# Two loads ahead of the opening barrier, with new load sizes and shares, in a streaming log-sum-exp

## The chip, the cores and the metric

The kernel runs on 1 core of one Trainium2 chip. The metric is the device time of one execution in microseconds (us). The profile's span, from the first instruction to the last landing, is about 1.8 us shorter than that time. Four comparisons were made, of which the last three ran on three different chips (batches 1 to 3 below). ACT is ScalarE, DVE is VectorE, SP the engine that issues the loads. A load lands when the last of the 16 DMA engines has reported its part; that report is called a completion here.

## The reference, cut to what matters

```python
x = np.random.randn(32, 512, 1024).astype(np.float32)
x_max = np.max(x, axis=-1, keepdims=True)
out = x_max.squeeze(-1) + np.log(np.sum(np.exp(x - x_max), axis=-1))     # (32, 512)
```

There are 16,384 rows of 1,024 floats. Laid over 128 partitions that is 128 rows to a partition. In this text "a row" is one such row on all partitions, 524,288 bytes. The kernel leaves the maximum out, which normally distributed inputs allow.

## The kernel before

Chunks of rows, one load each, are loaded one after the other into a ring of 51 rows. ACT takes the exponential. For the first rows of a chunk it does so in one call, and DVE sums them; for the others it does one call a row in the accumulating form, which sums by itself. A pair `(r, n)` in the list means r rows in the chunk, n of them summed on DVE.

```python
CHUNKS = [
    (4, 1), (15, 11), (16, 10), (16, 15), (16, 0), (14, 0), (12, 9), (9, 5), (7, 5), (5, 4),
    (4, 3), (3, 0), (2, 2), (2, 2), (1, 0), (1, 0), (1, 0),
]
...
    load(0)                                   # moved ahead of the opening barrier below
    n_early = len(body.instructions)
    nc.scalar.preload_act_table_set("natural_log_exp_and_others")
    for i, (r, n_dve) in enumerate(CHUNKS):
        if i:
            load(i)                           # waits until its place in the ring is free
        ...
        nc.scalar.wait_ge(landed[i], 16)
        if n_dve:
            nc.scalar.activation(out=ring[:, s : s + n_dve], in_=ring[:, s : s + n_dve], func=Exp)...
            nc.vector.wait_ge(act_done, acts)
            nc.vector.reduce_sum(out=sums[:, row : row + n_dve], in_=ring[:, s : s + n_dve], axis=AX)...
        for j in range(n_dve, r):
            nc.scalar.activation(out=ring[:, s + j], in_=ring[:, s + j], func=Exp,
                                 accum_out=sums[:, row + j : row + j + 1])...
    ...                                       # Ln of the sums, one store
```

The instructions recorded before `n_early` are put ahead of the barrier that opens the program.

The softmax here doesn't subtract the row's maximum and nothing guards it: scores larger than these inputs give would overflow.

## Time and profile before

| | before |
|---|---|
| time, median of the first 3 runs | 163.2 us (163.04 to 163.21) |
| span of the profiled run | 161.4 us |
| busy: ACT, DVE | 124.1 us, 72.9 us |
| load queue, share of the 16 DMA engines' span | 97.0% |
| last row lands, ACT takes it | 158.21, 158.34 |

The landings to a hundredth are the last of the 16 completions that the trace records for each load. How busy the three parts are, in 40 slices of 4 us, as tenths:

```profile
DVE  0030000029960699000799920000004999799874
ACT  3190006997089980999429999999999999999995
DMA  7999799989989989989989999999899999999990
```

ACT and DVE have holes; the DMA engines have none after the first slice. A digit below 9 in the DMA row comes from packets that lie over the edge of a slice: with each packet's time shared out between the slices that it covers, slices 2 to 39 come to 99% or more. The rest of the reading is in the prediction.

### The profile page before, as it was taken

What the parts mean: (1) busy time and instruction counts of PE and PEld (TensorE: products, weight loads), DVE (VectorE), ACT (ScalarE), POOL (GpSimd) and SP (SyncE); (2) the same over time, 40 slices, a digit from 0 to 9 for tenths busy, and PEclk for the clock granted to TensorE, in tenths of its full rate; (3) what the DMA queues carried; (4) which work ended last, traced back from release to release, by engine and by line L of the source; (5) the groups of instructions that cost most, each with busy time, mean ns of one, the idle gap of its engine ahead of it and who ended that gap; (6) DMA issues with size and microseconds to landing.
All of it is one profiled execution on the core that took longest, in us unless ns stands there. A gap on an engine that the chain in (4) does not pass through costs nothing.

```text
span 161.4 us, 212 instructions
## 1 busy us (share of the span) xinstructions
DVE 72.9 (45%) x11; ACT 124.1 (77%) x136; POOL 0.2 (0%) x4
## 2 busy tenths in 40 slices
DVE  0030000029960699000799920000004999799874
ACT  3190006997089980999429999999999999999995
POOL 0000000000000000000000000000000000000000
DMA  7999799989989989989989999999899999999990
GB/s 264 499 487 442 335 442 520 422 357 520 422 357 520 422 357 520 422 357 520 422 353 426 457 455 422 390 463 475 347 439 434 433 441 402 431 418 416 420 394 24
DMA packets 2593, 67.18 MB, mean 416 GB/s; under 512 B 288, under 2 KB 416, under 8 KB 800
## 3 DMA queue, kind: packets, MB, share of 16 engines
q1 hardware_dynamic: 2448, 67.11, 97.0%
q10 hardware_dynamic: 144, 0.07, 0.1%
q14 instruction: 1, 0.01, 0.0%
HBM read 67.11 MB, written 0.07 MB: 416 GB/s over the span
## 4 chain that ended last, share of the span: by engine, by line
ACT 52%; DMA 38%; DVE 7%; issue 1%
DMA ring<-in_x_dram 38%; ACT ring L127 30%; ACT ring L115 22%; DVE sums L120 7%; ACT res L92 0%
## 5 line engine op out<-in xcount | busy, mean ns | idle before, releaser
L120 DVE TENSOR_REDUCE sums<-ring 128x5 f32<-128x5120 f32 (+8 forms) x11 | 72.9, 6648 | 86.1 <-ACT ring L115 86.0
L115 ACT ACTIVATE ring<-ring 128x5120 f32<-128x5120 f32 (+8 forms) x11 | 59.3, 5395 | 29.6 <-DMA ring<-in_x_dram 29.6
L127 ACT ACTIVATE ring<-ring 128x1024 f32<-128x1024 f32 x61 | 63.4, 1041 | 5.3 <-DMA ring<-in_x_dram 5.3
L127 ACT ACTIVATION_READ_ACCUMULATOR ring<-ring 128x1 f32 x61 | 11.4, 187 | 0.0
L102 ACT ACT_TABLE_LOAD x1 | 1.3, 1283 | 0.8 <-PEq L181 0.8
L92 ACT ACTIVATE res<-sums 128x67 f32<-128x67 f32 (+1 forms) x2 | 0.5, 256 | 0.1
L181 POOL MEMSET const-bfloat16-1.0<- 128x1 bf16 x1 | 0.1, 101 | 0.0
L181 POOL MEMSET const-uint8-127<- 128x1 uint8 x1 | 0.1, 101 | 0.0
L181 POOL MEMSET const-float32-0.0<- 128x1 f32 x1 | 0.1, 98 | 0.2 <-issue 0.2
L181 POOL MEMSET const-float32-1.0<- 128x1 f32 x1 | 0.1, 98 | 0.0
## 6 DMA issues: line engine op xcount, KB each, us to landing
ring<-in_x_dram SPq DMA_DIRECT2D x1, 7680.0 KB, 24.9
ring<-in_x_dram SPq DMA_DIRECT2D x1, 7168.0 KB, 36.0
ring<-in_x_dram SPq DMA_DIRECT2D x1, 6144.0 KB, 21.6
ring<-in_x_dram SPq DMA_DIRECT2D x1, 4608.0 KB, 32.1
ring<-in_x_dram SPq DMA_DIRECT2D x2, 2048.0 KB, 26.3
ring<-in_x_dram SPq DMA_DIRECT2D x1, 3584.0 KB, 40.2
ring<-in_x_dram SPq DMA_DIRECT2D x1, 2560.0 KB, 44.4
ring<-in_x_dram SPq DMA_DIRECT2D x2, 1024.0 KB, 46.0
```

The source lines that it names most:

```text
L92: nc.scalar.activation(out=res[:, lo:hi], in_=sums[:, lo:hi], func=Ln).then_inc(act_done, 1)
L102: nc.scalar.preload_act_table_set("natural_log_exp_and_others")
L115: nc.scalar.activation(out=ring[:, s : s + n_dve], in_=ring[:, s : s + n_dve], func=Exp).then_inc(act_done, 1)
L120: nc.vector.reduce_sum(out=sums[:, row : row + n_dve], in_=ring[:, s : s + n_dve], axis=AX).then_inc(dve_done, 1)
L127: nc.scalar.activation(out=ring[:, s + j], in_=ring[:, s + j], func=Exp, accum_out=sums[:, row + j : row + j + 1],).then_inc(act_done, 1)
L181: nc = _bacc.Bacc("TRN2", target_bir_lowering=False, num_devices=1)
```

## The change

The intent: let the stream of loads open sooner, by a first load of two rows and a second one issued right behind it, and fit the sizes and shares to that.

```diff
 CHUNKS = [
-    (4, 1), (15, 11), (16, 10), (16, 15), (16, 0), (14, 0), (12, 9), (9, 5), (7, 5), (5, 4),
-    (4, 3), (3, 0), (2, 2), (2, 2), (1, 0), (1, 0), (1, 0),
+    (2, 1), (16, 13), (16, 10), (16, 1), (16, 0), (16, 12), (11, 9), (9, 5), (7, 6), (5, 2),
+    (4, 4), (3, 0), (2, 2), (2, 1), (1, 1), (1, 0), (1, 0),
 ]
@@
     load(0)
+    load(1)
     n_early = len(body.instructions)
@@
-        if i:
+        if i > 1:
             load(i)
```

## The prediction

> **What bounds the kernel now.** I read the queue table first, then the chain of work that ended last, the idle time of the engines, the groups kept apart by shape, and last the timeline of the final microseconds and the two loads that open and close the stream.
>
> ```profile
> span 161.4 us, 212 instructions
> DVE 72.9 (45%) x11; ACT 124.1 (77%) x136; POOL 0.2 (0%) x4
> q1 hardware_dynamic: 2448, 67.11, 97.0%
> ```
>
> The load queue holds the 16 DMA engines for 97.0% of 161.4, that is 156.6 us; ACT has 124.1 and DVE 72.9. The input stream is the largest load by far. That alone doesn't say what sets the end, so the chain (start, length, what), cut to the parts up to the point where it turns to ACT for good:
>
> ```profile
> 0.78 24.87 DMA ring<-in_x_dram
> 25.67 9.60 ACT ring L115
> 35.29 11.90 DVE sums L120
> 47.21 36.61 DMA ring<-in_x_dram
> 83.84 10.56 ACT ring L127 x21
> ```
>
> Read plainly, the chain says that the fifth load waited for a DVE reduction (47.21) and that ACT bounds all from 83.84 on. Both readings need a check. The fifth load is issued at 47.21, but the queue then still holds the fourth, which lands only when ACT starts on it at 64.50: that wait is hidden. And ACT's idle time before it, in the groups:
>
> ```profile
> L115 ACT ACTIVATE ring<-ring 128x15360 f32<-128x15360 f32 x1 | 13.0, 13002 | 4.4 <-DMA ring<-in_x_dram 4.4
> L115 ACT ACTIVATE ring<-ring 128x11264 f32<-128x11264 f32 x1 | 9.6, 9589 | 14.0 <-DMA ring<-in_x_dram 14.0
> L115 ACT ACTIVATE ring<-ring 128x10240 f32<-128x10240 f32 x1 | 8.7, 8736 | 5.7 <-DMA ring<-in_x_dram 5.7
> L120 DVE TENSOR_REDUCE sums<-ring 128x15 f32<-128x15360 f32 x1 | 16.2, 16153 | 12.8 <-ACT ring L115 12.8
> L120 DVE TENSOR_REDUCE sums<-ring 128x9 f32<-128x9216 f32 x1 | 9.8, 9753 | 29.6 <-ACT ring L115 29.6
> ```
>
> ACT waits for data before each of the first big chunks, so those starts are landings: 25.67 with 19 rows in, 83.84 (from the chain) with 67 rows in. The slope is 58.17/48 = 1.212 us for a row of 128x1024 floats, 524,288 bytes, or 433 GB/s. Last, the end. The final load's issue, its time to landing, and the timeline there:
>
> ```profile
> 112.46 0.45 SPq L84 DMA_DIRECT2D ring<-in_x_dram  x1
> DMA to landing us min/median/max: 45.8/45.8/45.8
> 158.34 1.04 ACT L127 ACTIVATE ring<-ring 128x1024 f32<-128x1024 f32 x1
> 159.28 0.19 ACT L127 ACTIVATION_READ_ACCUMULATOR ring<-ring 128x1 f32 x1
> 159.50 0.25 ACT L92 ACTIVATE res<-sums 128x61 f32<-128x61 f32 x1
> 159.78 0.37 ACTq L139 DMA_DIRECT2D out_dram<-res  x1
> ```
>
> The last row lands at 112.46 + 45.8 = 158.26 and ACT takes it at 158.34. So ACT arrives within 0.1 us of the data: the stream bounds the kernel, and ACT has been balanced to it. What follows (1.16 us to the logarithm, the logarithm, the store of 1.6 us) is fixed.
>
> **What the Trainium skill says.** "DMA: Bandwidth & Descriptors", section "Where 436 GB/s comes from", puts the ceiling of the 16 ports at 435 GB/s; the 433 above agrees, so no choice of load sizes can gain much. The same page, "Queues, rings and completion order", says each engine consumes its ring in order: a second load issued earlier queues behind the first. The trace agrees, loads land in order of issue. "ScalarE: Activation LUTs", section "What ACT_TABLE_LOAD costs", gives 186 ns + 0.833 ns an element with immediate operands, and an overlap of some 93 ns; for 9216 elements that is 7863, and the trace has 7867. "VectorE: DVE Perf Modes", section "The perf-mode tier table", has the reduction at 1x only; at its 0.96 GHz a row costs 1.067 us, and the trace has (16153 - 9753)/6 = 1067 ns.
>
> **The change, part by part.**
>
> *Both loads ahead of the barrier.* The second load is issued at 0.78 now, with the barrier in front of it. It will be at about 0.4, right after the first one's 0.37 us of issue. The barrier's end, and the table load behind it, come some 0.35 later, which is hidden: ACT then still waits for its first rows. In the windows of the first microseconds (us, the busy shares, then DMA share and GB/s last):
>
> ```profile
> 0.00:1.00 1.00, 0.00 (x0) 0.23 (x1) 0.20 (x4) 1.00 0.00 0
> 1.00:2.00 1.00, 0.00 (x0) 1.00 (x1) 0.00 (x0) 1.00 1.12 262
> 3.00:4.00 1.00, 0.00 (x0) 0.00 (x0) 0.00 (x0) 1.00 1.00 426
> ```
>
> Packets move from about 1 us after the first issue. By the same delay the second load's would be ready from 1.8 to 2.7 with the old issue time, 1.4 to 2.3 with the new. The first load of 4 rows keeps the engines until some 1.3 + 4 x 1.21 = 6.2; of 2 rows, until 3.7. Either way the second is queued in time. The stream's first byte depends on the first load alone, which doesn't move. Gain: 0.
>
> *Load sizes.* The running sum of rows is 2, 18, 34, 50, 66, 82, then 93, 102, 109, 114, 118, 121, 123, 125, 126, 127, 128: from the seventh load on it is the same as before, sizes included. The stream's end stays at 158.26. The new early landings come from the slope: second load at 24.5 (18 rows), third 43.9, fourth 63.3, fifth 82.6, sixth 83.84 + 15 x 1.212 = 102.0.
>
> *Buffers.* A load that waits for a free place costs only if it is issued after the queue has run dry. The tightest are those that need the sixth chunk's place, the first of them being the tenth load (5 rows). The sixth chunk's exponential of 12 rows starts at 102.0 and takes 10.35, the reduction 12 x 1.067 + 0.15 = 13.0, so the place is free at 125.4. By then the queue has work up to 109 rows: 1.3 + 109 x 1.212 = 133.4. Seven to eight us are left, less 1 to 2 for the first packets. The fifth load waits for a reduction of 13 rows to 49.8, against 62 when the queue runs dry. No starvation.
>
> *Shares.* A row by the accumulating form takes 1.04 from start to start; an exponential of n rows takes 0.853 n + 0.115 (start to start: 12.91 for 15 rows, 4.37 for 5). Before: 61 rows at 1.04, 67 rows in 11 calls. After: 62 rows at 1.04, 66 rows in 13 calls. ACT's sum grows by 1.04 - 0.853 + 2 x 0.115 = 0.42 us. Most of it falls where ACT waits. So I follow ACT from the last chunk it waits for. The sixth starts at 102.0 and takes 10.35 + 4 x 1.04, to 116.5; the seventh (9 + 2) takes 7.79 + 2.08, to 126.37; before, ACT came to the eighth at 126.25. Then 5 + 4 rows to 134.91 (134.80 before), 6 + 1 to 141.18 (141.25), 2 + 3 to 146.12 (145.80), 4 + 0 to 149.64 (149.49), 3 single rows to 152.76 (152.60), 2 to 154.58 (154.44), 1 + 1 to 156.59 (156.26), an exponential of 1 to 157.56 (157.30), a single row to 158.60. The last row starts at 158.60, not 158.34: +0.26. The stream is no longer quite last; ACT is 0.3 behind it. DVE's last single-row reduction ends near 159.4 behind the queue of the ones before it, just ahead of the accumulator's 159.7, so it adds nothing.
>
> Sum: 0 (barrier) + 0 (sizes) + 0 (buffers) + 0.26 (ACT's tail) on 163.2 gives 163.46; I say 163.4, as a first load of half the size may open the stream a little sooner.
>
> **The rivals.**
> 1. The early second load does pull the stream forward by the 0.4 us between 0.78 and 0.4, or the smaller first load makes the engines start more evenly, and everything anchored to landings comes forward with it: 163.46 - 0.4, about 163.0. For it: only 262 GB/s moved in the second microsecond, so the start isn't ideal, and somebody chose to do this. Against: full rate by the fourth microsecond with the late issue, and nothing after it for the second load to fill.
> 2. A place comes free too late, at the tenth load: the idle of the queue is then the loss, one for one. It needs DVE 6 us later than worked out, with durations that repeat to 0.1%; if it happened, 164 to 167.
> 3. DVE becomes the tail: its queue of reductions in the last 20 us is dense. It ends 0.3 before ACT by my sum; half a microsecond more on it gives 163.6 to 163.8.
>
> **Range and chances.** The three runs of before spread over 0.17. Rival 1 sets the low end, 162.7 with that spread; rivals 3 and a slip in ACT's tail the high end, 163.9. Two per cent is 3.3 us; faster by that would need the stream to end before 155, at 443 GB/s, above anything the trace shows. Slower by that needs rival 2. Within 2%: 0.98.
>
> **What would show it.** Right: the second issue near 0.4; ACT's start on the second chunk near 24.5 and on the sixth near 102.0; the last load landing within 0.2 of 158.26; ACT's last row starting 0.2 to 0.4 after that landing, with no idle of ACT behind 102. Wrong: an early shift common to all landings (rival 1), a hole in the DMA row of the page after 120 (rival 2), or the final logarithm waiting for DVE (rival 3).

## The result, and the profile after

The changed kernel took 163.51 us, median of 6 runs (163.37 to 163.93), against 163.24 (163.04 to 163.47) for the kernel before beside it. The ratio is 1.0021, 95% interval 1.0006 to 1.0036: the same within 2%. Ratios are the mean time of one kernel's fast runs over that of the other's in the same rounds, so not quite the ratio of the medians. The profiled run, at 163.83, is one of the two slowest of the six; its parts have to be read with that in mind.

The head of its page and its load queue:

```profile
span 162.0 us, 215 instructions
DVE 72.9 (45%) x13; ACT 124.2 (77%) x138; POOL 0.2 (0%) x4
q1 hardware_dynamic: 2448, 67.11, 96.8%
```

Nothing in the totals moved but the span. The start, in windows of one microsecond (DMA share and GB/s are the last two columns), and the second load's issue and landing (the issue line merges the first two):

```profile
1.00:2.00 1.00, 0.00 (x0) 0.75 (x1) 0.00 (x0) 1.00 0.71 205
2.00:3.00 1.00, 0.00 (x0) 0.53 (x1) 0.00 (x0) 1.00 1.02 426
0.00 0.85 SPq L84 DMA_DIRECT2D ring<-in_x_dram  x2
DMA to landing us min/median/max: 23.7/23.7/23.7
```

Both loads are out by 0.85; the second is issued at 0.42 and lands at 24.13. Full rate is there in the third microsecond. ACT's starts on the chunks it waited for are landings, from the timeline:

```profile
24.15 11.30 ACT L116 ACTIVATE ring<-ring 128x13312 f32<-128x13312 f32 x1 [17.21 <-DMA ring<-in_x_dram]
43.53 8.74 ACT L116 ACTIVATE ring<-ring 128x10240 f32<-128x10240 f32 x1 [4.96 <-DMA ring<-in_x_dram]
63.41 1.06 ACT L116 ACTIVATE ring<-ring 128x1024 f32<-128x1024 f32 x1 [4.91 <-DMA ring<-in_x_dram]
83.11 1.06 ACT L128 ACTIVATE ring<-ring 128x1024 f32<-128x1024 f32 x1 [3.07 <-DMA ring<-in_x_dram]
102.46 10.44 ACT L116 ACTIVATE ring<-ring 128x12288 f32<-128x12288 f32 x1 [2.33 <-DMA ring<-in_x_dram]
```

The steps are of 16 rows each: 19.38, 19.88, 19.70, 19.35 us, so 1.211, 1.242, 1.231, 1.209 us a row. The stream opens 0.35 earlier than my 24.5. It then loses 16 x (0.031 + 0.020) = 0.8 us in two loads, which nothing in the prediction foresees. The trace's single packets show how: at about 48, 58 and 68 us 13 of the 16 engines take 2.5 to 2.7 us for a packet of 64 KiB that otherwise takes 2.42. Last, the chain from the sixth chunk on (its first two pieces; all the others up to the final logarithm are ACT's), and the tail:

```profile
63.15 39.29 DMA ring<-in_x_dram
102.46 10.44 ACT ring L116
136.42 0.43 SPq L84 DMA_DIRECT2D ring<-in_x_dram  x1
DMA to landing us min/median/max: 22.2/22.2/22.2
158.89 1.04 ACT L128 ACTIVATE ring<-ring 128x1024 f32<-128x1024 f32 x1
160.06 0.26 ACT L92 ACTIVATE res<-sums 128x62 f32<-128x62 f32 x1
```

From 102.46 ACT has no hole. The last row lands at 158.65 (136.42 + 22.2, to the rounding of that view) and ACT takes it at 158.89, 0.24 later, where the kernel before takes it 0.12 after its landing. The span grew by 0.57; of that, 0.12 is ACT's lateness and 0.44 the later landing.

### The profile page after: what moved, and what is told of

The parts are those of the page before. It is cut to its first block, busy times and chain, and to the rows that moved or that the text cites. A ratio compares the mean times of both kernels' runs of the same rounds, so it can differ in the third digit from the quotient of the medians.

```text
span 162.0 us, 215 instructions
## 1 busy us (share of the span) xinstructions
DVE 72.9 (45%) x13; ACT 124.2 (77%) x138; POOL 0.2 (0%) x4
## 4 chain that ended last, share of the span: by engine, by line
DMA 50%; ACT 41%; DVE 7%; issue 0%
DMA ring<-in_x_dram 50%; ACT ring L116 28%; ACT ring L128 13%; DVE sums L121 7%; ACT res L92 0%
## 5 line engine op out<-in xcount | busy, mean ns | idle before, releaser
L121 DVE TENSOR_REDUCE sums<-ring 128x1 f32<-128x1024 f32 (+8 forms) x13 | 72.9, 5645 | 86.7 <-ACT ring L116 86.7
L116 ACT ACTIVATE ring<-ring 128x1024 f32<-128x1024 f32 (+8 forms) x13 | 59.6, 4591 | 31.7 <-DMA ring<-in_x_dram 31.7
L92 ACT ACTIVATE res<-sums 128x66 f32<-128x66 f32 (+1 forms) x2 | 0.5, 257 | 0.1
```

Source lines behind the costliest of these rows:

```text
L92: nc.scalar.activation(out=res[:, lo:hi], in_=sums[:, lo:hi], func=Ln).then_inc(act_done, 1)
```

## The experiments

Theory: the early issue and the sizes leave the stream as it was, and ACT's tail adds a little. Rivals: the stream opens earlier; the new sizes slow the stream. Because the first profile showed a gain and a loss inside the stream, most runs ask which of the two belongs to the change.

All profiles together. "Second chunk" is ACT's start on it; with 18 rows in, a row (1.21) has to be added to compare it with 19. "Late" is ACT's start on the last row less that row's landing.

| kernel | batch | median us | ratio | second chunk (rows) | last landing | late |
|---|---|---|---|---|---|---|
| before | first | 163.2 | | 25.67 (19) | 158.21 | 0.12 |
| after | first | 163.51 | 1.0021 | 24.15 (18) | 158.65 | 0.24 |
| after_again | 1 | 163.47 | 1.0018 | 24.07 (18) | 158.27 | 0.24 |
| early_only | 1 | 163.18 | 1.0003 | 25.59 (19) | 158.15 | 0.12 |
| sizes_only | 1 | 163.36 | 1.0011 | 24.13 (18) | 158.26 | 0.22 |
| old_tail | 1 | 163.16 | 1.0015 | 24.02 (18) | 157.81 | 0.17 |
| before_again | 2 | 163.58 | 0.9999 | 25.87 (19) | 158.96 | 0.12 |
| small_first | 2 | 163.43 | 0.9992 | 25.56 (19) | 158.49 | 0.13 |
| large_first | 2 | 163.42 | 0.9992 | 24.34 (18) | 158.26 | 0.24 |
| tail_heavy | 2 | 164.29 | 1.0043 | 24.30 (18) | 158.10 | 1.07 |
| before_third | 3 | 163.66 (one run) | | 25.63 (19) | 158.61 | 0.12 |
| after_third | 3 | 163.49 | 1.0012 | 24.17 (18) | 158.63 | 0.25 |
| thin_before | 3 | 162.48 | 0.9951 | 25.68 (19) | 158.06 | 0.02 |
| thin_after | 3 | 162.24 | 0.9940 | 24.16 (18) | 158.50 | 0.02 |

The kernel before had medians of 163.11, 163.59 and 163.28 beside the three batches. So chips alone differ by 0.5 us, more than the effect. In the 12 profiles of kernels that do the whole work, the time of the profiled run is the last landing plus "late" plus 4.93 to 4.96 us. So what is left of a difference in time, once the difference in "late" is taken off, is a difference in the end of the stream.

**after_again.** No edit.

> The changed kernel once more, unedited, to see which features of its one profile come back. In that profile the second load landed 0.3 us nearer the line of 1.21 us a row than before, and between 40 and 75 us the stream then lost 0.7 us that the kernel before does not lose. Theory 1 (the loss is a chance disturbance of the DMA engines): time 163.4 to 163.6, sixth chunk's start on ACT at 101.7 to 102.0 rather than 102.46, and no load slower than 1.22 us a row before the tail. Theory 2 (the loss belongs to the new load sizes): the fourth and fifth loads again take 1.23 to 1.24 us a row and the sixth chunk starts at 102.4 or later.

Measured: 163.47, six runs from 163.01 to 163.87, ratio 1.0018 (1.0004 to 1.0033). The sixth chunk starts at 102.07 and the fifth load takes 1.234 us a row. Both theories missed a part: a slow load came back, but one and not two, in the fifth and not the fourth, and its cost was about half. Neither "never" nor "always" holds.

**early_only.** The kernel before with the second load early:

```diff
     load(0)
+    load(1)
@@
-        if i:
+        if i > 1:
```

> The kernel before with nothing but the second load moved ahead of the barrier. Theory 1 (my prediction: the second load queues behind the first in any case): ratio 1.000 within 0.001, last load lands at 158.1 to 158.3, ACT's start on the second chunk at 25.6 to 25.7. Rival (the early issue is what brought the landings forward by 0.3 us): that start at 25.3 to 25.4, last landing near 157.9, time about 162.9, ratio 0.998.

Measured: ratio 1.0003 (0.9991 to 1.0015), last landing 158.15. The second chunk's start:

```profile
25.59 9.59 ACT L116 ACTIVATE ring<-ring 128x11264 f32<-128x11264 f32 x1 [13.96 <-DMA ring<-in_x_dram]
```

That is 0.08 before the first profile's 25.67, just under my 25.6 to 25.7 and well outside the rival's 25.3 to 25.4. The early issue alone brings at most 0.1 us.

**sizes_only.** The changed kernel with the second load behind the barrier again:

```diff
     load(0)
-    load(1)
@@
-        if i > 1:
+        if i:
```

> The changed kernel with the second load behind the barrier again; sizes and shares stay new. Theory 1 (the early issue is worth nothing): same as the changed kernel, ratio to before 1.001 to 1.003, second chunk's start on ACT near 24.2. Rival (early issue is worth 0.3 us): second chunk's start at 24.45 to 24.55 and the time 0.3 us above the changed kernel, ratio 1.004.

Measured: 163.36, ratio 1.0011 (0.9997 to 1.0025); the second load is issued at 0.77, and yet:

```profile
24.13 11.30 ACT L115 ACTIVATE ring<-ring 128x13312 f32<-128x13312 f32 x1 [17.33 <-DMA ring<-in_x_dram]
```

The start is where the changed kernel has it (24.07 on this chip), so the early issue isn't what brings it. Against early_only, a row added, it is 25.59 - 25.34 = 0.25 earlier: on this chip that belongs to the sizes. This run, too, has a slow load, its seventh, at 1.238 us a row. With that the seventh lands late, and the early start is gone by 115 us.

**old_tail.** The changed kernel with the shares of the last ten chunks of before:

```diff
-(9, 5), (7, 6), (5, 2), (4, 4), (3, 0), (2, 2), (2, 1), (1, 1), (1, 0), (1, 0)
+(9, 5), (7, 5), (5, 4), (4, 3), (3, 0), (2, 2), (2, 2), (1, 0), (1, 0), (1, 0)
```

> The changed kernel with the shares of the last ten chunks put back to those of before (ACT keeps one accumulating row less before the last four single rows). My sum gives ACT's start on the last row at 158.47 if the sixth chunk starts at 102.0, against 158.60 with the new shares and 158.34 before: so about 0.13 us under the changed kernel, ratio to before about 1.001. If ACT's tail is not what ends the kernel, it is equal to the changed kernel within 0.05 us.

Measured: 163.16, but runs from 162.92 to 164.15, ratio 1.0015 (0.9994 to 1.0035). As a time it tells nothing. In the profile ACT is 0.17 late, 0.07 less than with the new shares; my sum had 0.13. In its profile no load of 16 rows takes more than 1.221 us a row, and there the last row lands at 157.81, with a time of 162.92:

```profile
135.60 0.44 SPq L84 DMA_DIRECT2D ring<-in_x_dram  x1
157.98 1.04 ACT L128 ACTIVATE ring<-ring 128x1024 f32<-128x1024 f32 x1
```

So the early start can last to the end, when no slowing takes it back.

**before_again.** No edit.

> The kernel before, unedited, as a control: its second profile shows how far the stream's course differs between executions of one kernel. If the start of the stream is a property of the kernel, the second chunk starts on ACT at 25.6 to 25.7 as in the first profile and the engines' first and last completion of a load lie 0.75 to 0.85 us apart; if it is chance, 25.2 to 25.7 is possible. Time 163.0 to 163.3, ratio 1.000.

Measured: 163.58, ratio 0.9999. The time is above my 163.0 to 163.3, as that of the kernel before beside it is (163.59). The stream of its profile, the slowest of its five runs, is the worst of all: slowings of 6 to 11 engines at 6, 30 and 39 us, the second and third loads at 1.240 and 1.237 us a row, the last landing at 158.96. The second chunk starts at 25.87, outside what I had allowed, and from the third load on the engines' completions of one load lie 1.1 to 1.3 us apart instead of 0.8. The slowings aren't a mark of the new sizes.

**small_first.** The kernel before with another cut of the first two loads:

```diff
-    (4, 1), (15, 11),
+    (2, 1), (17, 11),
```

> The kernel before with the first two loads cut at 2 and 17 rows instead of 4 and 15; all sums from the second load on, all shares but one accumulating row, and the late second issue are those of before. Theory (the smaller first load alone brings all landings forward by 0.3 us): second chunk's start on ACT at 25.2 to 25.35, and if nothing is lost later, the last landing at 157.9 and the time 162.8 to 162.9, ratio 0.998. Rival (the gain is taken back by a common slowing of the DMA engines between 40 and 110 us, as in three of four profiles with the new sizes): same start, but the last landing at 158.1 to 158.6 and the time 163.0 to 163.5, with runs spread over more than 0.5 us.

Measured: 163.43 (163.27 to 163.58), ratio 0.9992 (0.9980 to 1.0005). The second chunk starts at 25.56, so neither expectation of the start was met, and the fourth load is slow (1.245 us a row), so the last landing is the rival's 158.49. The spread of its runs, 0.31, is under the rival's 0.5. One thing besides the cut differs: the load of 17 rows goes in 256 packets of 34,816 bytes, where the other large loads go in 128.

**large_first.** The changed kernel with another cut of the first two loads:

```diff
-    (2, 1), (16, 13),
+    (4, 1), (14, 13),
```

> The changed kernel with the first two loads cut at 4 and 14 rows instead of 2 and 16; the sums are those of the changed kernel from the second load on. Theory (first load's size sets the start): the second chunk starts on ACT at 24.45 to 24.55, not 24.1. If the even start of the small first load is also what makes the engines slow each other down later, this kernel shows no load over 1.22 us a row before the last ten, runs within 0.3 us, last landing 158.2 and the time 163.3 to 163.4 by ACT's tail alone. If the later slowing is independent of it, its runs spread like the changed kernel's, up to 163.9.

Measured: 163.42 (163.33 to 163.51), ratio 0.9992. The second chunk starts at 24.34, earlier than expected, and only 0.04 later than that of tail_heavy, which opens with two rows on the same chip. The fifth load took 1.228 us a row, but that is no common slowing: the packets show one engine alone held up at 72 us, by a fetch of instructions, and the completions of that load lie 0.95 us apart where those of the load before lie 0.65 apart. Apart from that the stream is even, as expected of the first case, and the last landing and lateness are as it said. One even execution doesn't show that the larger first load is the reason, since the kernel before, which also opens with four rows, had slowings in before_again. On this chip the gain of 0.25 us from the smaller first load is not seen; whether it is a matter of the chip or of the execution stays open.

**tail_heavy.** The changed kernel with five rows of the eighth chunk in the other form:

```diff
-(9, 5), (7, 6), (5, 2),
+(9, 0), (7, 6), (5, 2),
```

> The changed kernel with five rows of the eighth chunk moved from exponential plus reduction to the accumulating form. ACT's work in the tail grows by 9 x 1.04 - (4.37 + 4 x 1.04) = 0.83 us and DVE's falls by 5.5. Theory (ACT's tail is on the path, 0.25 behind the last landing): last row starts 1.0 to 1.1 us after the last landing, time 0.8 us above the changed kernel, ratio to before 1.006 to 1.008. Rival (the new tail is bound by the stream or by DVE's last reductions, ACT has slack): 0 to 0.3 us, ratio 1.002 to 1.004.

Measured: 164.29 (164.13 to 164.35). The ratio of 1.0043 is under the expected 1.006 to 1.008. That range took the changed kernel to be 1.002 against before; it was not run on this chip, where its nearest kin is below 1: large_first, the changed kernel but for its first cut, has 0.9992. Against that one, tail_heavy is 0.87 us slower, for 0.83 expected. Its tail:

```profile
135.88 0.43 SPq L84 DMA_DIRECT2D ring<-in_x_dram  x1
DMA to landing us min/median/max: 22.2/22.2/22.2
159.18 1.04 ACT L128 ACTIVATE ring<-ring 128x1024 f32<-128x1024 f32 x1
```

The last row lands at 158.10 and is taken 1.07 later: 0.24 and 0.83. DVE's busy time fell from 72.9 to 67.6 us and that bought nothing. ACT's tail is on the path, one for one.

**before_third.** No edit, one look.

> The kernel before, unedited, for a third profile, on the same chip as the next three. In its first profile the second load (19 rows) landed at 25.65, in its second at 25.85 on another chip, after a slowing at 6 us that all engines shared. ACT should again take the last row 0.12 to 0.13 us after it lands, whatever the stream does: that part is arithmetic on ACT's fixed durations.

Measured: 163.66, one run of unknown state. ACT is 0.12 late. The fourth load took 1.227 and the fifth 1.222 us a row, and the last landing is 158.61: the kernel before shows the same slowings at the same place as the changed one.

**after_third.** No edit.

> The changed kernel, unedited, for a third profile and a third comparison. Theory (two parts: ACT's tail costs a fixed 0.12 us, the rest of the difference is chance in the stream): last row taken 0.24 to 0.25 us after its landing; ratio to before between 0.999 and 1.002, not the same as on the first two chips. Rival (the new load sizes slow the stream themselves): ratio again at 1.002 or over, and a last landing at 158.3 or later.

Measured: 163.49 (163.31 to 163.81), ratio 1.0012 (0.9999 to 1.0025). ACT is 0.25 late. The last landing, 158.63, fits the rival's "158.3 or later", but before_third on the same chip has 158.61, so the two executions don't differ in it.

**thin_before.** The kernel before with every exponential and sum cut to 8 of 1,024 columns (a wrong result):

```diff
-                out=ring[:, s : s + n_dve], in_=ring[:, s : s + n_dve], func=Exp
+                out=ring[:, s : s + n_dve, 0:8], in_=ring[:, s : s + n_dve, 0:8], func=Exp
```

and the same on the input of the sum and on the accumulating form.

> The kernel before with every exponential and reduction cut to 8 of 1024 columns: a wrong result on purpose, all loads, waits and instruction counts kept, so that the stream runs with ACT and DVE nearly idle. If the common slowings of the DMA engines come from outside the core's own compute engines, they appear here too (a load of 16 rows over 1.22 us a row in some profile, runs spread by 0.3 us), and the time is that of before less 0.12 (no lateness) and 0.85 (the last row's exponential): 162.1 to 162.3 where before has 163.2. If ACT and DVE slow the stream, it ends 0.3 us or more earlier than that.

Measured: 162.48 (162.20 to 162.70), ratio 0.9951, and 0.80 under the 163.28 of before. I had written 162.1 to 162.3 for a before of 163.2; the median is a little over it. Its profile, the fastest of its six runs, has no slow load; the runs spread by 0.50. The last row lands at 158.06, a little before the earliest full kernel with these sizes (158.15). The medians are the better measure: they fell by 0.80, while the time from the last landing to the end, by the profiles, shrank by 0.92 (from 5.06 to 4.14). So with ACT and DVE nearly idle the stream doesn't end earlier.

**thin_after.** The changed kernel thinned in the same way.

> The changed kernel thinned in the same way: the early issue and the load sizes alone, without ACT's tail. My prediction for these two parts was zero: within 0.1 us of the thinned kernel before. Rival 1 (the smaller, earlier start brings the stream forward): 0.3 to 0.4 us faster than it, ratio to before lower by 0.002. Rival (the new sizes slow the stream): 0.2 us or more slower than it.

Measured: 162.24 (162.00 to 162.64), ratio 0.9940, so 0.24 us under thin_before by the medians. That lies between my zero and rival 1's 0.3 to 0.4, and the runs of the two overlap (162.20 to 162.70 and 162.00 to 162.64): not settled. It speaks against the rival by which the new sizes slow the stream by 0.2 us or more. Its chunk starts, with ACT 11% and DVE 2% busy:

```profile
43.52 0.27 ACT L116 ACTIVATE ring<-ring 128x80 f32<-128x80 f32 x1 [18.50 <-DMA ring<-in_x_dram]
63.14 0.21 ACT L116 ACTIVATE ring<-ring 128x8 f32<-128x8 f32 x1 [18.21 <-DMA ring<-in_x_dram]
82.73 0.21 ACT L128 ACTIVATE ring<-ring 128x8 f32<-128x8 f32 x1 [16.51 <-DMA ring<-in_x_dram]
102.09 0.28 ACT L116 ACTIVATE ring<-ring 128x96 f32<-128x96 f32 x1 [15.90 <-DMA ring<-in_x_dram]
```

The steps of 16 rows are 19.62, 19.59 and 19.36 us: two slow loads (1.226, 1.224 us a row); the seventh, of 11 rows, takes 1.231. All this while hardly anything but the loads is running. So the slowings don't need ACT's and DVE's work.

## Why the prediction was right or wrong

The time was right: 163.4 said, range 162.7 to 163.9, 163.51 measured. That it came so close is partly luck: the prediction put the whole growth of 0.26 on ACT's tail, which gave 0.12, and a later landing that it didn't foresee gave the rest. Two of its own signs failed in the first profile, where the sixth chunk starts at 102.46 (102.0 said) and the last landing is 0.39 from 158.26 (0.2 allowed); in after_again both are met. Point by point:

- **The barrier part (gain 0): right.** The second issue is at 0.42, and early_only and sizes_only put its worth at under 0.1 us. The queue was never empty for it to fill.
- **The load sizes (gain 0, end at 158.26): right for the end within its scatter, wrong for the start.** The second chunk starts at 24.15, not 24.5, and in all three profiles of the changed kernel between 24.07 and 24.17. Rival 1 named both halves of the change, for 0.4. The early issue is not the cause; the sizes are, with 0.25 in batch 1, and likewise 0.25 (after_third) and 0.31 (thin_after) against their kernels of before in batch 3, there together with the early issue. The first load's size alone was tried in batch 2 only, and no gain from it is seen there. The packets hint at how a gain can arise: each engine's first packet took 0.41 to 0.54 us longer than its later ones with four rows in the first load, 0.13 to 0.46 with two. That this makes the gain isn't shown. The end is nevertheless the old one. The mean of the last landings is 158.41 over the six profiles with the sizes of before (small_first among them) and 158.31 over the eight with the new ones, and each set spreads over 0.8 to 0.9 us.
- **What was missing: slowings of nearly all DMA engines.** The prediction took 1.212 us a row as fixed. In 9 of the 14 profiles at least one early load of 11 to 17 rows took over 1.225 us a row, and in 8 of these several to all engines slow down together (large_first is the ninth). The places differ between executions; both kernels have it, and it comes with ACT and DVE idle too. It took back the early start in most profiles; in those of old_tail and tail_heavy it didn't. One regularity: slowings of nine engines or more that follow each other in one profile mostly lie 9.8 to 10.0 us apart, or twice that (47.5, 57.4, 67.4 in the first profile after; 54.7, 64.5, 74.3, 84.2 in after_again, with one more at 71.9). Four packets of 64 KiB take 9.7, so a beat from outside and every fourth packet can't be told apart here. The cause stays open: none of the changes tried, sizes, early issue or idle ACT and DVE, makes the slowings come or go, and what else ran on the chip is not in the record.
- **The buffers (no starvation): right.** The tenth load is issued at 125.91, for 125.4 said, with the sixth chunk 0.46 later than said; the ninth load's packets kept the engines busy to 134.0 at least. The fifth is issued at 49.53, for 49.8. That DVE's durations repeat to 0.1% is too fine, but makes no odds: equal reductions of the profile before took 5475 and 5487 ns, 2277 and 2286 ns.
- **ACT's tail (+0.26): right mechanism, half the size.** Lateness went from 0.12 to 0.24, so +0.12, in all profiles with the new shares within 0.03. The mis-sized term is the 0.115 us of an exponential call. I fitted it on calls that had waited for a landing. Back to back they take less, as these lines of the changed kernel show:

```profile
126.82 4.45 ACT L116 ACTIVATE ring<-ring 128x5120 f32<-128x5120 f32 x1
131.18 1.04 ACT L128 ACTIVATE ring<-ring 128x1024 f32<-128x1024 f32 x1
135.33 5.31 ACT L116 ACTIVATE ring<-ring 128x6144 f32<-128x6144 f32 x1
140.54 1.04 ACT L128 ACTIVATE ring<-ring 128x1024 f32<-128x1024 f32 x1
```

  Start to start that is 4.36 for 5 rows and 5.21 for 6, where the formula has 4.38 and 5.23. Eight such calls lie behind the sixth chunk: 8 x 0.02 = 0.16. The last row was to be taken 0.34 after its landing, and 0.34 less some 0.16 is close to the 0.24 measured, with the 0.04 that was lost by rounding the landing of before. The Trainium skill ("ScalarE: Activation LUTs", section "What ACT_TABLE_LOAD costs") had the term: by its figures, 186 ns less the 93 ns of overlap, the estimate is 0.093, and the lines above give 4.36 - 5 x 0.853 = 0.095. I quoted it and used my fit. Apart from this, the prediction's count of all shares is wrong: both kernels have 61 rows in the accumulating form and 67 in calls, so ACT's sum grows by two calls, about 0.2, and not 0.42 (busy: 124.1 and 124.2); and the seventh load has 11 rows, not the 12 of before. Neither enters the 0.26, which was followed chunk by chunk.
- **DVE's end (rival 3): right that it adds nothing.** Its last reductions end at 155.05 + 4.54 = 159.59, before the accumulator read that ends at 160.03.
- **The sum.** 0.12 of the difference to before is shown, by the profiles and one for one by tail_heavy. The ratios 1.0021, 1.0018 and 1.0012 make 0.2 to 0.3 us. The rest, 0.1 to 0.2 us, is a later end of the stream, and I don't give it a cause: it has no sign that all chips share. With the lateness taken off, the ratios of large_first and tail_heavy, both with the new sizes, leave a stream that ends 0.25 earlier than that of before, and those of the thinned pair one that ends 0.18 earlier, each with a doubt of some 0.2. No version was shown to beat both kernels: old_tail and small_first each have an interval that contains 1.

## What to carry to other kernels

When one stream of transfers fills the whole time, look first for two things: when its first packet moves, and how long the last piece of work takes after the last landing. The end of the stream of one unchanged kernel, before, lay between 158.21 and 158.96 in three profiles here, so one profile doesn't tell a gain from chance. An earlier issue, behind work that was already queued, was worth under 0.1 us here. Work on a balanced engine behind the stream cost its lateness at the last landing (0.83 us later, 0.87 us slower), so compare kernels by that difference within one profile, which repeated to 0.03 us here, and not by times that scatter over 0.5 us. And fit the cost of a call from calls in the same situation, back to back or after a wait.

## What the Trainium skill lacked or had wrong

- "DMA: Bandwidth & Descriptors", "Where 436 GB/s comes from": the ceiling of 435 GB/s fits the best loads, 1.205 to 1.207 us a row or 434 to 435 GB/s. No page tells of the slowings: loads at over 1.225 us a row, up to 1.245, with several to all engines slow at once, in 8 of 14 profiles, and in one of them with all but the loads nearly idle.
- The same page, "Latency and other measured facts", gives about 600 ns to the first byte for a DMA issued from the sync engine. Here the first packet starts 0.98 to 1.01 us after the start of the first issuing instruction, in all 14 profiles, and 0.62 to 0.64 after its end. Counted from the end the two agree; what the page lacks is from where it counts.
- The same page gives no cost for a small load in a queue that is full: the first two of the three loads of one row took 1.27 to 1.29 us each, against 1.21 for a row of a large one.
- "ScalarE: Activation LUTs" is right on the exponential, and has no cost for the accumulating form: 1.04 us a row start to start, where its figures for a plain exponential, 186 + 853 - 93 ns, make an estimate of 0.95.
- "Runtime: NRT & Kernel Launch", "Instruction fetch mechanics", calls the cost of crossing an instruction block mostly hidden. In every profile one fetch of 8,192 bytes (at 72.4 us after, 89.1 before) takes 0.31 to 0.34 us on one DMA engine in the midst of the loads, and a load packet that starts at its end takes 0.24 to 0.33 us longer than others of its size. In large_first, where the spread of the completions went from 0.65 to 0.95 us there, the landings behind it came 0.3 us later against the line of 1.21 us a row; in the first profile of before nothing is seen of it.
